# A decoder layer on one core: attention loads issued one per step, and late modulation computed by halves of 512 columns

## The chip, the cores and the metric

The kernel runs on one core of one Trainium2 chip. The metric is device time of one execution, in microseconds (us); smaller is better. The core has TensorE (PE, with its weight loads shown apart as PEld), VectorE (DVE), ScalarE (ACT), GpSimd (POOL) and SyncE (SP). SP issues nearly all the transfers between HBM and on-chip memory in this kernel; its queue is in order, so a row that waits holds every row behind it.

## The reference

The layer has 2048 tokens of width 1024, in float32, for a single sequence. Cut to what matters here:

```python
mod = silu(c) @ w_ada + b_ada          # w_ada is 1024 x 6144
shift_a, scale_a, gate_a, shift_m, scale_m, gate_m = split(mod, 6)
h = rms_norm(x, g_attn) * (1 + scale_a) + shift_a
q_f, k_f, v_f, q_s, k_s, v_s, f_logit = split(h @ w_in)
o_fox = forgetting_attention(q_f, k_f, v_f, log_sigmoid(f_logit + b_fgate))
o_sb = stick_breaking_attention(q_s, k_s, v_s)
mix = concat(head_rms_norm(o_fox), head_rms_norm(o_sb))
x = x + gate_a * (mix @ w_out)
h = rms_norm(x, g_mlp) * (1 + scale_m) + shift_m
x = x + gate_m * (conv_gated_mlp(h))
return rms_norm(x, g_final)
```

There are 8 forgetting ("fox") heads and 8 stick-breaking ("sb") heads of 64 columns, both causal. The six parts of `mod` are used at different times. The first two are needed before anything else. `gate_a` scales the output projection, so it can be multiplied into `w_out` beforehand. `scale_m`, `shift_m` and `gate_m` are wanted only after attention. The change touches how these last four are computed while attention runs.

## The kernel before, in words

Values that need full precision are split into a high and a low part, and a product is three matmuls (high by high, high by low, low by high).

**Units.** Attention is cut into 32 units, in this order: for sb and then for fox, four pairs of heads `p`, and for each pair four blocks `tb` of 512 tokens. A unit's attention (`attend`, L692) is the main stream. The projection of a later unit (`proj`, L455 on) runs as a filler between its steps: `follow` advances it as far as a table `pace` asks. The projection reads the normalised input in eight tiles of 512 KB for each block of tokens (the loads at L468, `hp<-hs`, matmuls at L342), multiplies them with the input weights and writes q, k and v back to HBM.

**Loads of a unit.** Once a unit's projection is done, `load_unit` (L351 to L365) issues the nine loads of its attention: four of Q (L362), four of K (L363) and one of V (L364). All nine come at one step.

**Late modulation.** From unit 12 on, `late_mod` (L757) is a second filler with 3 of its steps per unit. For each of four 1024-column parts of `w_ada` it takes a tile `wsum` and then, for each of the eight row blocks, a further tile `w`. It loads 512 KB (L776), and by halves of 512 columns scales them on ScalarE (L782) and adds them to `wsum` on GpSimd (L783); the first block is scaled on GpSimd straight into `wsum` (L780). A matmul with ones (L790) then sums over the partitions. For the two gates the bias row comes by a load of its own into a tile `gt` (L787), which VectorE adds (L791). For the first gate `fold_out` (L743) multiplies `w_out` by it, splits the product and writes it to HBM. The second gate is stored from `gt` by one transfer (L796, `gate_m`).

**The ring.** All these tiles, `wsum`, `w`, `gt`, the raw and split tiles of `fold_out`, and the eight `hs` tiles of a projection, come from one ring of ten buffers of 512 KB (`h_tile`, L156; `wide` is the same buffer seen as 1024 columns). A load into a buffer waits until all users of its previous content are done.

**Order.** The rows of each engine are put in order by a planner that simulates the program. What a row waits for on the chip is decided by semaphores, and the order of rows on an engine is fixed.

## Time and profile before

| | us |
|---|---|
| median of 3 runs (lowest, highest) | 2948.92 (2948.36, 2949.31) |
| profiled execution, span | 2941.4 |
| TensorE busy in it | 2867.8 (97%) |
| VectorE, ScalarE, GpSimd busy | 2179.5, 1686.0, 901.1 |

The profiled execution's own span is 2941.4 us; the device time of the runs, 2948.92 us, also holds what lies around the span, 7.5 us. A sum made in the profile is therefore carried over by adding 7.5 us.

Rows name the source line, the engine, the operation, the tile written and the tile read. "hp" is a tile of the ring, "hs" the normalised input in HBM. "SPq" rows are the issues of transfers by SP. A wait "A <- B" says that engine row A stood idle until B released it. The PEclk column is the TensorE clock that was granted, as a share of full speed.

### The profile page before, as it was taken

To read this page: it belongs to the slowest core of one execution; us is meant where nothing else is said; L and a number is where in the kernel's file an instruction comes from. 1 tells how busy PE (TensorE), PEld (TensorE's weight loads), DVE (VectorE), ACT (ScalarE), POOL (GpSimd) and SP (SyncE) were. 2 spreads that over 40 slices of the span, in tenths; PEclk is the share of its full clock that TensorE was granted. 3 is DMA by queue.
4 is the path that set the end of the run, shared out by engine and by line. 5 is a ranking of instruction groups with operands and counts; after the bars stand their busy time and mean duration, and the time that the engine had idled before them with its cause. 6 is when DMAs were issued, how large, how long until landed. Compare 5 with 4: busy or idle time off the path is not lost.

```text
span 2941.4 us, 45922 instructions
## 1 busy us (share of the span) xinstructions
PE 2867.8 (97%) x15772; PEld 2459.7 (84%) x15772; DVE 2179.5 (74%) x3464; ACT 1686.0 (57%) x3187; POOL 901.1 (31%) x967
## 2 busy tenths in 40 slices
PE   8999999999999999999999999999999999999998
PEld 7888888888988988888888788888788888888887
DVE  5787778877886656658843788888998888575476
ACT  5776767677776656658744554444444445433342
POOL 0431322243032423231213344444254543142200
PEclk8999999999999999999999999999999999999999
DMA  9749756867469794794537775554754444975644
GB/s 293 255 139 321 236 188 207 301 211 229 162 212 356 269 277 139 232 323 140 182 120 233 245 232 128 130 136 129 236 132 125 130 130 132 309 257 185 216 158 151
DMA packets 348346, 601.89 MB, mean 205 GB/s; under 512 B 34672, under 2 KB 178800, under 8 KB 348112
## 3 DMA queue, kind: packets, MB, share of 16 engines
q1 hardware_dynamic: 324208, 558.06, 57.7%
q0 software_dynamic: 10880, 20.97, 4.3%
q10 hardware_dynamic: 13024, 19.93, 1.9%
q8 instruction: 124, 2.03, 0.3%
q14 instruction: 110, 0.90, 0.1%
HBM read 420.77 MB, written 177.02 MB: 203 GB/s over the span
## 4 chain that ended last, share of the span: by engine, by line
PE 46%; DMA 3%; DVE 2%; SPq 1%; ACT 1%; issue 1%; POOL 0%; DVEq 0%; ACTq 0%; POOLq 0%
PE ps_o L1315 19%; PE ps_t L1315 7%; PE ps_o L1614 6%; PE ps_t L1614 3%; PE ps_bc L1614 3%; PE ps_o L912 1%; PE ps_pv L615 1%; DMA r<-rstd 1%; PE ps_bc L912 1%; PE ps_pt L606 1%; PE ps_o L1609 1%; DMA wo<-wos 1%; DMA hm<-hf_m 1%; SPq L895 1%; DVE op L46 1%
## 5 line engine op out<-in xcount | busy, mean ns | idle before, releaser
L1315 PE MATMUL ps_o<-op,wu 128*128 128x512 f32 x2592 | 608.0, 389 | 2.0 <-DVE snap L1366 1.5
L1315 PEld LDWEIGHTS ps_o<-op,wu 128*128 128x128 f32 x2592 | 486.2, 188 | 103.9 <-DVE snap L1366 1.9
L611 DVE TENSOR_TENSOR at<-ps_pt,at 128x512 fp32r<-128x512 f32 (+1 forms) x576 | 366.1, 652 | 100.2 <-ACT at L610 97.3
L636 DVE TENSOR_TENSOR_SCAN a<-r,a 128x512 f32<-128x512 f32 (+2 forms) x320 | 368.3, 1167 | 77.8 <-ACT a L631 39.9
L342 PE MATMUL ps_pj<-hp,w_qk 128*128 128x512 f32 x1512 | 411.2, 403 | 14.5 <-DMA hp<-hs 12.9
L610 ACT ACTIVATE at<-ps_pt 128x512 fp32r<-128x512 f32 (+1 forms) x576 | 318.5, 576 | 139.1 <-PE ps_pt L606 123.1
L615 PE MATMUL ps_pv<-at,V 128*128 128x256 f32 x2216 | 386.8, 292 | 9.3 <-DVE at L611 4.2
L615 PEld LDWEIGHTS ps_pv<-at,V 128*128 128x128 f32 x2216 | 320.9, 190 | 39.8 <-DVE at L611 11.4
L342 PEld LDWEIGHTS ps_pj<-hp,w_qk 128*128 128x128 f32 x1512 | 275.4, 190 | 71.0 <-DMA hp<-hs 16.2
L45 ACT ACTIVATE wu<-wuraw 128x512 fp32r<-128x512 f32 x204 | 128.9, 632 | 248.5 <-PE ps_o L1315 190.1
L596 PE MATMUL ps_qk<-K,Q 128*128 128x512 f32 (+2 forms) x640 | 265.7, 416 | 5.6 <-ACT a L631 3.3
L413 PE MATMUL ps_pj<-w_v,hp 128*128 128x256 f32 (+1 forms) x1536 | 236.6, 288 | 2.1 <-DVE hp L422 1.6
L597 PE MATMUL ps_qk<-K,Q 128*128 128x512 f32 (+2 forms) x640 | 235.7, 369 | 0.0
L1315 PE MATMUL ps_t<-op,wu 128*128 128x512 f32 x888 | 220.8, 390 | 1.0 <-DVE op L46 1.0
L413 PEld LDWEIGHTS ps_pj<-w_v,hp 128*128 128x128 f32 x1536 | 209.0, 189 | 10.9 <-DVE q L373 1.5
L630 ACT ACTIVATE r<-ps_qk 128x512 f32<-128x512 f32 (+2 forms) x320 | 173.1, 541 | 58.2 <-PE ps_qk L597 55.5
L46 DVE TENSOR_TENSOR wu<-wuraw,wu 128x512 fp32r<-128x512 f32 x204 | 189.6, 930 | 18.1 <-ACT wu L45 16.7
L1315 PEld LDWEIGHTS ps_t<-op,wu 128*128 128x128 f32 x888 | 166.4, 188 | 36.5 <-DVE op L46 1.8
L606 PE MATMUL ps_pt<-edge,a 128*128 128x128 f32 x1088 | 185.1, 274 | 8.4 <-DVE a L636 7.8
L1614 PE MATMUL ps_o<-op 128*128 128x512 f32 x840 | 191.5, 389 | 0.0
L1614 PEld LDWEIGHTS ps_o<-op 128*128 128x128 f32 x840 | 157.7, 188 | 32.7
L679 ACT ACTIVATE p<-p,mn 128x128 f32<-128x128 f32 (+15 forms) x128 | 153.9, 1203 | 53.3 <-DVE mn L675 52.2
(342 smaller groups left out, 5237.6 us busy)
## 6 DMA issues: line engine op xcount, KB each, us to landing
hp<-hs SPq DMA_DIRECT2D x224, 512.0 KB
wuraw<-in_w_up_dram SPq DMA_DIRECT2D x80, 512.0 KB
ra<-g SPq DMA_DIRECT2D x136, 256.0 KB
rb<-in_w_down_dram SPq DMA_DIRECT2D x108, 256.0 KB
g<-u SPq DMA_DIRECT2D x80, 256.0 KB
hs<-hp SPq DMA_DIRECT2D x32, 512.0 KB
hp<-in_w_ada_dram SPq DMA_DIRECT2D x32, 512.0 KB
qk_fox<-q SPq DMA_DIRECT2D x32, 512.0 KB
```

Source lines behind the costliest of these rows:

```text
L46: (lo_engine or nc.gpsimd).tensor_sub(lo, src, f(hi))
L342: nc.tensor.matmul(acc, w[kt][:, a, n], h[:, bb], start=kt == 0 and i == 0, stop=kt == KT - 1 and i == 2)
L413: nc.tensor.matmul(av[:, t * width:(t + 1) * width], hts[kt][:, a, tok], w[1][kt][:, bb, 0:width], start=kt == 0 and m == 0, stop=kt == KT ...
L596: nc.tensor.matmul(b[:, :cw], Q[:, hl, 0, qcols], K[:, hl, :cw], start=True, stop=False)
L597: marks.append(nc.tensor.matmul(b[:, :cw], Q[:, hl, 1, qcols], K[:, hl, :cw], start=False, stop=True).ins)
L606: nc.tensor.transpose(b[:, i * P:(i + 1) * P], blk(kts[kk], qi), ident)
L610: copies = [nc.scalar.activation(at[:, 0, lo:], b[:, lo:], AF.Copy).ins, nc.vector.tensor_sub(at[:, 1, lo:], b[:, lo:], f(at[:, 0, lo:])).ins]
L611: nc.vector.tensor_sub(at[:, 1, lo:], b[:, lo:], f(at[:, 0, lo:])).ins]
L615: m = nc.tensor.matmul(o[:, 0:2 * P], V[kt // 4][:, kt % 4, hl, :], rhs, start=first and kk == 0 and w == 0, stop=last and kk == 1 and w == 1)
L636: nc.vector.tensor_tensor_scan(rev, r[:, 0:need][:, ::-1], rev, 0.0 if right[qi] is None else right[qi][:, 0:1], ALU.mult, ALU.add)
L1315: nc.tensor.matmul(b, w[:, p, j], o[:, q], start=first and i == 0, stop=last and i == 2, skip_group_check=True)
L1614: nc.tensor.matmul(b, a[:, p, t * P:(t + 1) * P], w[:, q], start=first and i == 0, stop=last and i == 2, skip_group_check=True)
```

## The change

Two things change. `load_unit` no longer issues its nine transfers but puts them in a list; `arrive`, called at every attention step, issues one of them, or all that remain when few steps are left in the unit (`n - m` not above the list's length plus six). Late modulation works on 512 columns at a time: one ring tile (`two_`) holds `wsum` in its first half and `w` in its second, all eight loads (256 KB each) go into the same `w`, and the gate's bias and the gate itself take `w`'s place after them. `fold_out` is called once for each half, uses the `wsum` half for the raw `w_out` rows, and takes one further tile at a time for the split. The filler gets 5 steps per unit rather than 3, since it now has about 90 steps in place of 55.

```diff
--- before.py
+++ after.py
@@ -359,10 +359,16 @@
             rows = slice(h * HD, (h + 1) * HD)
             for r in range(2):
                 half = slice(r * HD, (r + 1) * HD)
-                nc.sync.dma_start(f(Q[half, h]), src[rows, 0])
-                nc.sync.dma_start(f(K[half, h]), src[rows, 1, r])
-        nc.sync.dma_start(f(V), vs[kind][p][tb])
+                arriving.append((f(Q[half, h]), src[rows, 0]))
+                arriving.append((f(K[half, h]), src[rows, 1, r]))
+        arriving.append((f(V), vs[kind][p][tb]))
         res.append((Q, K, V))
+
+    arriving = []
+
+    def arrive(n):
+        for _ in range(min(n, len(arriving))):
+            nc.sync.dma_start(*arriving.pop(0))
 
     def finish_proj(kind, p, tb, aq, w, hts, ak=None):
         direct = (kind, p) == ("sb", 0)
@@ -740,18 +746,15 @@
         nc.sync.dma_start(os_[mp][tb], oT)
         yield
 
-    def fold_out(gt):
+    def fold_out(n, gt, raw):
+        sl = slice(n * TB, (n + 1) * TB)
         for kt in range(KT):
-            raw = wide()
-            nc.sync.dma_start(raw, w_out[kt * P:(kt + 1) * P, :])
-            for n in range(2):
-                sl = slice(n * TB, (n + 1) * TB)
-                nc.vector.scalar_tensor_tensor(raw[:, sl], raw[:, sl], cols[:, R_GF + kt:R_GF + kt + 1], gt[:, sl],
-                                               ALU.mult, ALU.mult)
-                w = h_tile()
-                split(w[:, 0], w[:, 1], raw[:, n * TB:(n + 1) * TB])
-                nc.sync.dma_start(wos[kt][:, :, n * TB:(n + 1) * TB], f(w))
-                yield
+            nc.sync.dma_start(raw, w_out[kt * P:(kt + 1) * P, sl])
+            nc.vector.scalar_tensor_tensor(raw, raw, cols[:, R_GF + kt:R_GF + kt + 1], gt, ALU.mult, ALU.mult)
+            w = h_tile()
+            split(w[:, 0], w[:, 1], raw)
+            nc.sync.dma_start(wos[kt][:, :, sl], f(w))
+            yield
 
     def late_mod():
         cr = f(h_tile())[0:2 * NFULL + 1].rearrange("p a (b n) -> p (a b) n", b=4)[:, 0:4]
@@ -770,37 +773,37 @@
         yield
         late = ((2, 0), (5, 1), (3, None), (4, None))
         for part, gate in late:
-            wsum = wide()
-            for kt in range(KT):
-                w = wide()
-                nc.sync.dma_start(w, w_ada[kt * P:(kt + 1) * P, part * D:(part + 1) * D])
-                for n in range(0, D, 512):
-                    sl = slice(n, n + 512)
+            for n in range(2):
+                two_ = f(h_tile())
+                wsum, w = two_[:, 0], two_[:, 1]
+                sl = slice(part * D + n * TB, part * D + (n + 1) * TB)
+                for kt in range(KT):
+                    nc.sync.dma_start(w, w_ada[kt * P:(kt + 1) * P, sl])
                     if kt == 0:
-                        nc.gpsimd.tensor_scalar_mul(wsum[:, sl], w[:, sl], cs[:, 0:1])
+                        nc.gpsimd.tensor_scalar_mul(wsum, w, cs[:, 0:1])
                     else:
-                        nc.scalar.activation(w[:, sl], w[:, sl], AF.Copy, scale=cs[:, kt:kt + 1])
-                        nc.gpsimd.tensor_add(wsum[:, sl], wsum[:, sl], w[:, sl])
-                yield
-            if gate is not None:
-                gt = wide()
-                nc.sync.dma_start(gt, b_ada[0:1, part * D:(part + 1) * D].to_broadcast([P, D]))
-                for n in range(2):
+                        nc.scalar.activation(w, w, AF.Copy, scale=cs[:, kt:kt + 1])
+                        nc.gpsimd.tensor_add(wsum, wsum, w)
+                    yield
+                if gate is not None:
+                    nc.sync.dma_start(w, b_ada[0:1, sl].to_broadcast([P, TB]))
                     b = pt()
-                    nc.tensor.matmul(b, ones, wsum[:, n * 512:(n + 1) * 512], start=True, stop=True)
-                    nc.vector.tensor_add(gt[:, n * 512:(n + 1) * 512], b, gt[:, n * 512:(n + 1) * 512])
+                    nc.tensor.matmul(b, ones, wsum, start=True, stop=True)
+                    nc.vector.tensor_add(w, b, w)
                     yield
-                if gate == 0:
-                    yield from fold_out(gt)
+                    if gate == 0:
+                        yield from fold_out(n, w, wsum)
+                    else:
+                        nc.sync.dma_start(gate_m[:, n * TB:(n + 1) * TB], w)
                 else:
-                    nc.sync.dma_start(gate_m, gt)
-            else:
-                cb = pt()
-                for d in range(KT):
-                    nc.tensor.matmul(cb[:, d:d + 1], wsum[:, d * P:(d + 1) * P], ones[:, 0:1], start=True, stop=True)
-                i = 1 if part == 3 else 0
-                nc.vector.tensor_add(mod_m[:, i], cb[:, 0:KT], cols[:, R_BA + part * KT:R_BA + (part + 1) * KT])
-                yield
+                    cb = pt()
+                    for d in range(KT // 2):
+                        nc.tensor.matmul(cb[:, d:d + 1], wsum[:, d * P:(d + 1) * P], ones[:, 0:1], start=True, stop=True)
+                    i = 1 if part == 3 else 0
+                    d0 = n * KT // 2
+                    c0 = R_BA + part * KT + d0
+                    nc.vector.tensor_add(mod_m[:, i, d0:d0 + KT // 2], cb[:, 0:KT // 2], cols[:, c0:c0 + KT // 2])
+                    yield
         nc.vector.scalar_tensor_tensor(mod_m[:, 0], mod_m[:, 0], 1.0, cols[:, R_GM:R_GM + KT], ALU.add, ALU.mult)
         yield
 
@@ -859,7 +862,7 @@
                       base + (total - base) * (done + weight(units[i]) * m / n) / span if i >= START else 0)
 
     LAG, ENDQ = 12, 16
-    LATE, PER = 12, 3
+    LATE, PER = 12, 5
     START, STOP = 3, 30
 
     HT = 2 * P
@@ -1020,6 +1023,7 @@
     weights["sb", 0], results["sb", 0] = load_w("sb", 0), []
     first_block(weights["sb", 0])
     load_unit(*units[0], results["sb", 0])
+    assert not arriving
     loaded_units = [1]
     close_pool("mod")
     sx = open_pool("sx", side="right")
@@ -1063,6 +1067,7 @@
             if nxt and projected[1] > i + 1 and loaded_units[0] == i + 1:
                 loaded_units[0] += 1
                 load_unit(*nxt, results[nxt[:2]])
+            arrive(1 if n - m > len(arriving) + 6 else len(arriving))
 
         interleave(attend(kind, p, tb, results[kind, p], Fbs), n, [(lm if i >= LATE else None, PER, False), (tail, 17 + IDLE if nxt is None else 13, True)], follow)
         while nxt and loaded_units[0] == i + 1:
```

In the changed kernel the line numbers are higher: the loads of a unit are at L371, of `hs` at L474, of `w_ada` at L781, the bias at L789 and the store of `gate_m` at L797.

The following rows are from SP's order, in which "x4" stands for four transfers in a row and the number behind a name tells tiles apart. First the place where late modulation begins (sb units), before:

```order
L316 DMA raw_qk_8414<-in_w_in_dram 128x2x128
L776 DMA hp_8615<-in_w_ada_dram 128x1024
L394 DMA qk_sb3_3_8202<-q2_8319 128x1024
L316 DMA raw_v_8419<-in_w_in_dram 128x256
L316 DMA raw_v_8424<-in_w_in_dram 128x256
L776 DMA hp_8671<-in_w_ada_dram 128x1024
L316 DMA raw_v_8429<-in_w_in_dram 128x256
L316 DMA raw_v_8434<-in_w_in_dram 128x256
```

and with the change:

```order
L316 DMA raw_qk_8414<-in_w_in_dram 128x2x128
L781 DMA hp_8614<-in_w_ada_dram 128x512
L474 DMA hp_9201<-hs1_0_68 128x1024
L400 DMA qk_sb3_3_8202<-q2_8319 128x1024
L316 DMA raw_v_8419<-in_w_in_dram 128x256
L781 DMA hp_8614<-in_w_ada_dram 128x512
L316 DMA raw_v_8424<-in_w_in_dram 128x256
L316 DMA raw_v_8429<-in_w_in_dram 128x256
L316 DMA raw_v_8434<-in_w_in_dram 128x256
```

Before, each load of `w_ada` goes to a new ring buffer; now every load goes to `hp_8614`, and an `hs` load has come between.

Next the place where attention turns to fox pair 1 and the projection of fox pair 2, token block 1, begins (tiles `hs1`), before:

```order
L363 DMA K_13512<-qk_fox1_2_12345 64x512 x3
L653 DMA Fb_13244<-fs_243 128x1024
L362 DMA Q_13260<-qk_fox1_1_11941 64x1024 x4
L440 DMA vs_fox2_0_222<-q2_13722 128x1024
L440 DMA vs_fox3_0_226<-q2_13723 128x1024
L363 DMA K_13989<-qk_fox1_3_12746 64x512 x4
L468 DMA hp_14078<-hs1_5_73 128x1024
L468 DMA hp_14107<-hs1_6_74 128x1024
L468 DMA hp_14112<-hs1_7_75 128x1024
L776 DMA hp_14199<-in_w_ada_dram 128x1024
```

and with the change, where the first `hs1` load is the row of `hp_14006`:

```order
L781 DMA hp_13439<-in_w_ada_dram 128x512
L371 DMA K_14660<-qk_fox2_0_13236 64x512 x2
L316 DMA raw_qk_16521<-in_w_in_dram 128x2x128
L371 DMA V_14018<-vs_fox1_3_221 128x1024
L316 DMA raw_qk_16526<-in_w_in_dram 128x2x128
L316 DMA raw_qk_16531<-in_w_in_dram 128x2x128
L474 DMA hp_14006<-hs1_0_68 128x1024
L789 DMA hp_12309<-in_b_ada_dram 128x512
L474 DMA hp_14011<-hs1_1_69 128x1024
L474 DMA hp_14057<-hs1_2_70 128x1024
L474 DMA hp_14062<-hs1_3_71 128x1024
L474 DMA hp_14093<-hs1_4_72 128x1024
```

Before, the sixth to eighth `hs1` tiles stand behind Q, two stores of v and four K loads; now the K and V loads stand ahead of the whole block, mixed with loads of `w_ada`, and the bias row of the gate stands behind the first `hs1` load.

Last the end of the loads for the projection of fox pair 2, token block 3 (tiles `hs3`), before, where `gate_m` is the store of the second gate:

```order
L653 DMA Fb_15445<-fs_243 128x1024
L362 DMA Q_15461<-qk_fox2_1_14178 64x1024 x3
L363 DMA K_15722<-qk_fox2_2_14948 64x512
L796 DMA gate_m_248<-hp_14928 128x1024
L363 DMA K_15722<-qk_fox2_2_14948 64x512
L468 DMA hp_15772<-hs3_7_91 128x1024
L364 DMA V_15463<-vs_fox2_1_223 128x1024
L776 DMA hp_15866<-in_w_ada_dram 128x1024
```

and with the change:

```order
L781 DMA hp_15551<-in_w_ada_dram 128x512
L371 DMA Q_14659<-qk_fox2_0_13236 64x1024 x4
L446 DMA vs_fox2_2_224<-q2_15346 128x1024
L446 DMA vs_fox3_2_228<-q2_15347 128x1024
L474 DMA hp_15785<-hs3_6_90 128x1024
L474 DMA hp_15790<-hs3_7_91 128x1024
L781 DMA hp_15551<-in_w_ada_dram 128x512
```

Before, the eighth tile `hs3_7` follows the store of `gate_m`, whose tile is a ring buffer; now both halves of that store come earlier in the order, and the eighth `hs3` tile follows the seventh. Ahead of the block stand single-tile loads of `w_ada` (`hp_15551`), four of them in a row:

```order
L797 DMA gate_m_248<-hp_13439 128x512
L386 DMA qk_fox2_2_14970<-q2_14967 128x1024
L781 DMA hp_15551<-in_w_ada_dram 128x512
L400 DMA qk_fox2_2_14970<-q2_15130 128x1024
L781 DMA hp_15551<-in_w_ada_dram 128x512 x4
L474 DMA hp_15595<-hs3_0_84 128x1024
L474 DMA hp_15600<-hs3_1_85 128x1024
L474 DMA hp_15677<-hs3_2_86 128x1024
```

On SP there are 1824 issue rows in place of 1781: the loads of `w_ada` go from 32 to 64, of `w_out` from 8 to 16, of the bias from 2 to 4, and `gate_m` is stored in two pieces. The number of rows on TensorE, ScalarE and GpSimd is the same; VectorE has two more. The first row that differs is 3815 of 15555 on TensorE, 955 on ScalarE, 199 on GpSimd and 224 on SP.

## The prediction

> **What bounds the kernel now.** I read the page first, then what TensorE waits for in the whole span and in the stretch where late modulation runs beside fox attention, then the timeline at its longest gaps, the stage windows around them, and SP's queue, which feeds them.
>
> ```profile
> span 2941.4 us, 45922 instructions
> PE 2867.8 (97%) x15772; PEld 2459.7 (84%) x15772; DVE 2179.5 (74%) x3464; ACT 1686.0 (57%) x3187; POOL 901.1 (31%) x967
> ```
>
> TensorE is busy for 97% of the span. Of the other 73.6 us only what lies in this stage can be had, plus what lies hidden in busy time at a lower clock. The waits in the whole span, then those from 880 to 1500 us:
>
> ```profile
> PE ps_pj L342 <- DMA hp<-hs: 12.9, 8, 6.0
> PE ps_pt L606 <- DVE a L636: 7.8, 16, 1.5
> PE ps_pv L615 <- DVE at L611: 4.2, 9, 1.0
> ...
> PE ps_pj L342 <- DMA hp<-hs: 9.9, 3, 6.0
> PE ps_bc L615 <- ACT at L610: 1.4, 3, 0.6
> ```
>
> So three waits for `hs` tiles make 9.9 us, and two of them are nearly all of it. The timeline has them, with the idle time before each in brackets; the row between is the last projection ahead of the second:
>
> ```profile
> 1052.80 2.93 PE L342 MATMUL ps_pj<-hp,w_qk 128*128 128x512 f32 x6 [6.01 <-DMA hp<-hs]
> ...
> 1155.19 1.66 PE L342 MATMUL ps_pj<-hp,w_qk 128*128 128x512 f32 x6 [0.47 <-DMA hp<-hs]
> 1208.81 2.93 PE L342 MATMUL ps_pj<-hp,w_qk 128*128 128x512 f32 x6 [3.40 <-DMA hp<-hs]
> ```
>
> After each the clock is down. The windows give length, busy time with counts of PE, PEld, DVE, ACT and POOL, granted clock, DMA share and GB/s:
>
> ```profile
> 1052.80:1056.40 3.60, 3.60 (x11) 2.91 (x12) 0.00 (x0) 0.00 (x0) 0.00 (x0) 0.50 1.06 308
> 1208.80:1213.60 4.80, 4.79 (x16) 4.21 (x17) 1.55 (x3) 3.11 (x10) 0.74 (x1) 0.50 0.76 290
> 880.00:900.00 20.00, 19.99 (x123) 17.17 (x121) 14.43 (x38) 13.83 (x32) 6.72 (x10) 1.00 1.04 374
> 1020.00:1040.00 20.00, 20.00 (x136) 17.94 (x135) 13.53 (x34) 14.87 (x29) 8.33 (x10) 1.00 1.00 285
> 1160.00:1180.00 20.00, 19.80 (x142) 18.05 (x142) 18.64 (x51) 16.60 (x27) 3.39 (x6) 1.00 0.04 15
> ```
>
> Half clock for 3.60 and 4.80 us costs 1.8 and 2.4 us of work. The stalls are then worth 6.0 + 1.8 = 7.8 and 3.4 + 2.4 = 5.8, together 13.6 us, 0.46% of the span. This is the pool from which a gain can come.
>
> [...]
>
> Why were the tiles late? SP's issues around the stalls (start, time, line, transfer, count):
>
> ```profile
> 1041.12 4.49 SPq L363 DMA_DIRECT2D K<-qk_fox  x4
> 1045.92 2.54 SPq L468 DMA_DIRECT2D hp<-hs  x3
> ...
> 1087.76 0.73 SPq L787 DMA_DIRECT2D hp<-in_b_ada_dram  x1
> ...
> 1154.17 1.04 SPq L316 DMA_DIRECT2D raw_qk<-in_w_in_dram  x2
> 1167.74 0.34 SPq L740 DMA_DIRECT2D os<-oT  x1
> 1181.77 1.72 SPq L653 DMA_DIRECT2D Fb<-fs  x2
> 1189.81 3.01 SPq L363 DMA_DIRECT2D K<-qk_fox  x5
> ...
> 1198.70 0.33 SPq L796 DMA_DIRECT2D gate_m<-hp  x1
> 1199.07 0.44 SPq L363 DMA_DIRECT2D K<-qk_fox  x1
> 1200.74 0.33 SPq L468 DMA_DIRECT2D hp<-hs  x1
> ```
>
> The first stall is a load issued too late on full transfer engines (share 1.00 from 1020 on): the three `hs` tiles are issued behind four K loads and land only at 1052.80, 6.9 us after the first of them. The second is the ring: `gt` was taken with the bias load at 1087.76 and left with the `gate_m` store at 1198.70, 111 us later; the next issue but one is the eighth `hs` tile, on which TensorE waits. In between the transfer engines were all but idle (0.04 from 1160 to 1180), so nothing but a buffer and an in-order queue stood in the way.
>
> **The change part by part.**
>
> *The ring, second stall.* Before, late modulation holds `wsum`, `gt` and a `w` in flight, each a whole buffer; now one buffer at a time for half a part (two when two halves overlap), and no `gt`. In SP's order all eight `hs3` tiles stand together, and `gate_m`'s stores come before them. Both causes are gone: minus 3.4 + 2.4 = 5.8 us. If the tile is late anyway for the queue, 0 to 5.8 comes back; I take all of it as won.
>
> *The unit's loads, first stall.* Spreading holds only where the unit has more steps left than loads plus six. Before unit 12 it does next to nothing: up to there SP's order differs by one K load that moved behind a store of q. From the fox pairs on, the K, V and Q loads stand mixed with `w_ada` loads and ahead of the `hs1` block rather than inside it. Ahead of `hs1_0` there are still K, V and raw weights. TensorE waits on no K, Q or V load in the rows shown, so moving them earlier costs nothing by itself; what matters is whether the block of eight `hs` loads lands in time. Bounds: the stall is gone (minus 7.8) or it moves to the block's first tile at about its old size (0). The queue shows 4.49 us for four K loads; taking those out from between would leave 6.0 - 4.5 = 1.5 us of the 6.0, but the block's 4 MB at the 285 GB/s shown is 14.7 us, so its last tiles are less safe than its first. I keep about two thirds of the stall, 5.0 us, as the cost of a smaller stall here or at the next pair, and so win 2.8.
>
> *The stage in the sb units,* where late modulation starts:
>
> ```profile
> 560.00:640.00 80.00, 77.53 (x463) 66.68 (x462) 60.36 (x76) 56.72 (x123) 14.84 (x19) 1.00 0.74 255
> 640.00:720.00 80.00, 73.45 (x474) 63.42 (x473) 58.16 (x78) 59.02 (x134) 38.50 (x44) 1.00 0.79 232
> ...
> PE ps_pt L606 <- DVE a L636: 3.6, 7, 1.1
> PE ps_pv L615 <- DVE at L611: 2.9, 6, 1.0
> PE ps_pj L342 <- DMA hp<-hs: 2.4, 4, 1.0
> ```
>
> TensorE idles 9.0 us in these 160 us; the last three rows are its waits from 600 to 880. Only the third is about the ring; I take 2.0 of its 2.4 as won. Bounds: 4 lost, if moved rows meet the vector chain at a worse place (about what the first row cost already), to 7 won.
>
> *The chain of single loads.* Late modulation's rows:
>
> ```profile
> L776 SPq DMA_DIRECT2D hp<-in_w_ada_dram x32: 328/333/2012, 629.7 to 1308.4; - x32
> L782 ACT ACTIVATE hp<-hp,cs x56: 705/714/744, 643.8 to 1320.8; 128x512 f32<-128x512 f32 x56
>   DMA hp<-in_w_ada_dram: 23.5, 17
> L783 POOL TENSOR_TENSOR hp<-hp x56: 1267/1293/2204, 644.6 to 1322.3; 128x512 f32<-128x512 f32 x56
> L780 POOL TENSOR_SCALAR hp<-hp,cs x8: 1557/1567/1574, 637.1 to 1251.3; 128x512 f32<-128x512 f32 x8
>   DMA hp<-in_w_out_dram: 2.2, 3
> ```
>
> Scaling and adding are of the same shape and number, so their busy time does not change. What changes is the wait: `w` is one buffer, so a load is issued only after the add before it, and ScalarE meets each of 56 loads singly instead of every second instruction of a pair. It waited 23.5 us in 17 of them; queued behind such a wait are the exponentials and scalings of attention (L610) for TensorE. If exposures double, ScalarE waits another 23.5. What reaches TensorE is bounded by 0 and that 23.5. The nearest row is TensorE's own: 1.4 us for L610 from 880 to 1500. I take it once more, with the extra waits of VectorE's `w_out` loads (2.2 us before) for another 0.6: plus 2.0. For the range I use 0 and 8, a third of the upper end, since ScalarE is busy for 57%.
>
> *SP and the transfers.* 43 more issues at 333 ns are 14 us over the 690 us in which late modulation runs, in a queue that stood idle in the stretch above; hidden. Uncovered, four more issues ahead of an `hs` block are 1.3 us. Value 0, bounds 0 to 2.
>
> [...]
>
> *Sum:* -5.8 - 2.8 - 2.0 + 2.0 + 0 = -8.6 us. From 2941.4 that is 2932.8, and with the 7.5 us by which the runs' median stands above the span, 2940.3; I write 2940.5. All units after about 1320 us are untouched, and late modulation's last add at 1322.3 is not on TensorE's way, so what is won remains won.
>
> **The rivals.**
>
> *Exchange.* The two stalls go and others of their kind come: the order now puts the whole `hs1` block behind K, V and `w_ada` loads, and the same at the turn to fox pair 2. For it: full transfer engines at 1020 to 1060, which the change relieves of nothing (the same bytes). Against it: the second stall had idle transfer engines. Two stalls of 7.8 and 5.8 become two of 5 to 8 us: 2948.9 - 13.6 + 13 = 2948. The variant in which the change does not do what it says, the loads not being spread where it counts, ends at the same figure.
>
> *The single-buffered chain holds SP (slower).* Each load waits for GpSimd's add, and SP holds everything behind it. One link is the landing, the scaling and the add. The first load above was issued at 629.7 and used at 637.1, so a link is up to 7.4 + 0.7 + 1.3 = 9.4 us. 64 + 16 such links would take 752 us against the 693 from 629.7 to 1322.3. The place is SP's order before the `hs3` block: four loads into `hp_15551` in a row, 4 x 9.4 = 38 us in which no `hs` load can be issued. Attention alone covered 52 us between 1156 and 1208 before; that cover is now cut into shorter pieces. From a link of about 8 us on (4 x 8 = 32) it decides. Priced by the stall of the same kind, three places of this form (ahead of `hs1`, `hs2`, `hs3`) cost 3 x 7.8 = 23.4 where 13.6 was paid before: 2948.9 + 9.8, about 2959. Against it: links in an idle stretch should be shorter, and two chains overlap in parts of the order.
>
> **How the numbers follow.** I give the forecast 0.48, the exchange 0.27, the chain 0.25. The forecast's own range, from its bounds, is 2933 to 2946 (all of the first stall won and 7 in the sb stage gives 2930.6; 0 there and the chain's 8 gives 2949; neither end is likely whole). With the exchange and most of the chain's case the range is 2931 to 2958. A measurement of this kernel can tell about 0.2% from no change, 5.9 us: faster is below 2943.0, slower above 2954.8. Faster holds most of the forecast's case (0.41) and a little of the exchange (0.06): 0.47. Same: 0.07 + 0.18 + 0.04 = 0.29. Slower: 0.03 of the exchange and 0.21 of the chain: 0.24.
>
> **What would show it.** Right: no wait of L342 on `hp<-hs` above 2 us between 1150 and 1250 and a granted clock of 1.00 there; at most one such wait near 1040 to 1060, below 5 us; ScalarE's wait for `w_ada` grown without TensorE's wait on L610 growing by more than 2 us. Exchange: new waits of 3 us or more on `hp<-hs` at other times with windows at 0.50 behind them. The chain: SP's waits for the `w_ada` buffer on GpSimd's add far above what they were, and `hs` issues right behind them. The forecast is wrong altogether if the time is gained or lost outside 620 to 1330 us, or if TensorE waits on late modulation's own matmuls.

## The result: slower, 1.0042 of the time before

The changed kernel takes 2965.31 us in the median of 7 runs (2950.13 to 2968.64), the kernel before 2948.92 (2948.35 to 2956.09). The ratio is 1.0042, with a 95% interval of 1.0025 to 1.0060. So about 12 us were lost by the ratio, 16 by the medians, where 8 had been forecast as a gain.

The page of the changed kernel, its first lines:

```profile
span 2963.6 us, 45975 instructions
PE 2879.3 (97%) x15772; PEld 2466.2 (83%) x15772; DVE 2170.2 (73%) x3466; ACT 1685.6 (57%) x3187; POOL 906.6 (31%) x967
```

TensorE executes as many instructions as before, yet is busy 11.5 us longer (2879.3 against 2867.8) and idle 10.7 us longer (84.3 against 73.6). The mean granted clock over the span fell from 0.993 to 0.990, which makes some 8.6 of the 11.5 us. That part is chance: in a second pair of traces, shown further down, the clock is 0.988 before and 0.991 with the change, and TensorE is busy equally long (2877.6 and 2877.4 us). What both pairs share is more idle time, in the second pair 80.7 us against 75.7. The profiled execution of the changed kernel took 2965.31 us with a span of 2963.6, so only 1.7 us lie around a span. The 7.5 us that the prediction put there were for the most part chance: the profiled execution of before was a quick one.

TensorE's waits in the changed kernel (what waited, for what, total us, times, longest):

```profile
PE ps_pj L342 <- DMA hp<-hs: 9.4, 8, 2.4
PE ps_pt L612 <- DVE a L642: 7.5, 16, 1.5
PE ps_pj L419 <- ACT w_v L45: 5.3, 2, 2.8
PE ps_pv L621 <- DVE at L617: 5.2, 9, 1.8
```

No stall of 6 us is left, and the longest wait for an `hs` tile is 2.4 us. But their sum is still 9.4 us (12.9 before), and a wait for ScalarE's split weights is new. The timeline has these places, and one more, ahead of 922.27 us:

```profile
922.27 1.48 PE L621 MATMUL ps_pv<-at,V 128*128 128x256 f32 x9 [1.99 <-DVE oT L744]
...
1047.78 0.50 PE L419 MATMUL ps_pj<-w_v,hp 128*128 128x256 f32 x2 [2.80 <-ACT w_v L45]
1054.47 0.50 PE L419 MATMUL ps_pj<-w_v,hp 128*128 128x256 f32 x2 [2.54 <-ACT w_v L45]
...
1257.74 1.63 PE L342 MATMUL ps_pj<-hp,w_qk 128*128 128x512 f32 x3 [2.43 <-DMA hp<-hs]
```

The windows of the changed kernel (length, busy us with counts of PE, PEld, DVE, ACT and POOL, granted clock, DMA share, GB/s) from 890 to 1000, and around the two stalls of before:

```profile
890.00:1000.00 110.00, 104.71 (x640) 90.34 (x639) 80.81 (x211) 70.04 (x131) 27.72 (x38) 0.97 0.74 252
1040.00:1060.00 20.00, 14.19 (x99) 13.03 (x99) 6.94 (x14) 9.55 (x23) 6.05 (x9) 0.91 0.92 231
1150.00:1250.00 100.00, 99.06 (x645) 88.36 (x644) 54.53 (x137) 54.82 (x97) 25.54 (x33) 1.00 0.70 236
1250.00:1265.00 15.00, 12.57 (x84) 11.53 (x84) 7.64 (x17) 7.42 (x16) 1.47 (x2) 0.89 1.05 246
```

and of before, for the first:

```profile
890.00:1000.00 110.00, 109.92 (x670) 96.80 (x669) 74.53 (x178) 66.76 (x128) 33.60 (x44) 1.00 0.91 329
```

From 890 to 1000 us, where TensorE had been busy without a gap, it now idles 5.3 us and runs at a mean clock of 0.97 (110 x 0.03 = 3.3 us more). These are the first units of fox attention, whose rows are short. What fills TensorE there is shown by the same windows for the projection's bank `ps_pj` alone (PE, PEld, DVE, ACT), before:

```profile
890.00:1000.00 110.00, 56.73 (x224) 39.50 (x223) 6.88 (x10) 5.96 (x10) 1.00 0.91 329
```

and after:

```profile
890.00:1000.00 110.00, 29.38 (x114) 20.73 (x115) 3.95 (x6) 3.24 (x6) 0.97 0.74 252
```

224 projection matmuls stood between the attention's steps, now 114. The longest gap there, the 1.99 us for `oT`, has a second side, in VectorE's timeline:

```profile
921.13 0.75 DVE L753 SCALAR_TENSOR_TENSOR hp<-hp,cols 128x512 f32<-128x512 f32 x1 [1.69 <-DMA hp<-in_w_out_dram]
921.80 0.41 DVE L744 TENSOR_TENSOR oT<-ps_pv,o 64x256 f32<-64x256 f32 x1
```

L753 is a row of `fold_out`, a part of late modulation. VectorE waited 1.69 us in it for a load of `w_out`, and the row that TensorE needed stands right behind it in VectorE's order. In the kernel before, ten such rows run in this stretch and none of them waits.

Two explanations went to the experiments. **Theory A**: the single `w` buffer; its loads hold ScalarE's and SP's in-order queues (VectorE's, shown above, was not in it). **Theory D**: the order that the planner makes of the changed program uses the projection up too early, and where it is missing the chain of attention (scores, maximum, exponential, sum) lies open. Beside them stands **theory B**, that the spread loads cost, and **theory C**, chance in the landing of transfers.

### The profile page after: what moved, and what is told of

The parts are those of the page before. It is cut to its first block, busy times and chain, and to the rows that moved or that the text cites. A ratio compares the mean times of both kernels' runs of the same rounds, so it can differ in the third digit from the quotient of the medians.

```text
span 2963.6 us, 45975 instructions
## 1 busy us (share of the span) xinstructions
PE 2879.3 (97%) x15772; PEld 2466.2 (83%) x15772; DVE 2170.2 (73%) x3466; ACT 1685.6 (57%) x3187; POOL 906.6 (31%) x967
## 5 line engine op out<-in xcount | busy, mean ns | idle before, releaser
L342 PE MATMUL ps_pj<-hp,w_qk 128*128 128x512 f32 x1512 | 414.8, 403 | 13.6 <-DMA hp<-hs 9.4
L642 DVE TENSOR_TENSOR_SCAN a<-r,a 128x512 f32<-128x512 f32 (+2 forms) x320 | 366.1, 1161 | 80.7 <-ACT a L637 39.8
L342 PEld LDWEIGHTS ps_pj<-hp,w_qk 128*128 128x128 f32 x1512 | 274.1, 190 | 69.7 <-DMA hp<-hs 13.0
L602 PE MATMUL ps_qk<-K,Q 128*128 128x512 f32 (+2 forms) x640 | 267.3, 419 | 10.7 <-ACT a L637 4.5
L46 DVE TENSOR_TENSOR op<-ra,op 128x512 fp32r<-128x512 f32 x144 | 108.5, 759 | 95.9 <-ACT op L45 93.3
```

The source lines that it names most:

```text
L46: (lo_engine or nc.gpsimd).tensor_sub(lo, src, f(hi))
L342: nc.tensor.matmul(acc, w[kt][:, a, n], h[:, bb], start=kt == 0 and i == 0, stop=kt == KT - 1 and i == 2)
L602: nc.tensor.matmul(b[:, :cw], Q[:, hl, 0, qcols], K[:, hl, :cw], start=True, stop=False)
L642: nc.vector.tensor_tensor_scan(rev, r[:, 0:need][:, ::-1], rev, 0.0 if right[qi] is None else right[qi][:, 0:1], ALU.mult, ALU.add)
```

## The experiments

All ratios are against runs of the kernel before on the same chip, with 95% intervals.

**How far chance goes.** The changed kernel and the kernel before were run once more, unchanged.

> The changed kernel once more, for a second trace. It lost about 5.5 us against before ahead of late modulation's start, where the order of rows is the same on every engine but for one K load, about 13 us in the stage of late modulation and about 4 us in the MLP. If chance in the landing of transfers makes the parts ahead and behind (theory C), they are at other places or gone in this trace, and the losses in the stage of late modulation stay: ScalarE waits for w_ada around 50 us in all, and the two TensorE stalls on ScalarE's w_v of 2.5 to 2.8 us come again. If all is set by the order, the same gaps stand at the same places and the time is 2965 within 2 us.

> The kernel before once more, for a second trace. The stalls at 1052 (about 6 us) and 1208 (about 3.4 us) should stand again if they are set by the order; idle time from 890 to 1000 us should be below 1 us again. Parts outside late modulation (300 to 600 us, and the MLP after 1720) show how far chance alone moves them, 2 to 4 us each.

Measured: the change again 2962.60 us, 1.0050 (1.0032 to 1.0068). The copy of before 2953.88 us, 1.0012 (0.9999 to 1.0025), with a span of 2953.3 in its profiled execution against 2941.4 in the first. So differences of 0.1% are nothing here, and one trace of this kernel can differ from another by 12 us. In the second trace of the change the losses that count stand again: 6.6 us idle from 890 to 1000 at a clock of 0.97, the two waits on `w_v` (shorter, 1.9 and 1.7 us), 50.8 us of ScalarE's waits for `w_ada`. In the second trace of before the two stalls stand again (4.53 us at 1063, 3.33 us at 1219), and 890 to 1000 us is again without a gap (109.92 busy). Theory C is out as a cause, though it blurs every small difference.

**The spread loads alone.** The edit on the kernel before is the list and `arrive` only:

```diff
-                nc.sync.dma_start(f(Q[half, h]), src[rows, 0])
-                nc.sync.dma_start(f(K[half, h]), src[rows, 1, r])
+                arriving.append((f(Q[half, h]), src[rows, 0]))
+                arriving.append((f(K[half, h]), src[rows, 1, r]))
...
+            arrive(1 if n - m > len(arriving) + 6 else len(arriving))
```

> The kernel before with only the spreading of a unit's nine loads. Theory A (late modulation's single buffer holds ScalarE's and SP's queues): the time of before within 0.2%, 2943 to 2955, and ScalarE's wait for w_ada stays at 20 to 30 us. Theory B (the spread loads fall into bursts at the turns between fox pairs and make the weights and hs tiles late): slower by 8 us or more, with stalls near the turns. The second stall of before (ring held by the gate tile) should stay under both.

Measured: 2962.21 us, 1.0036 (1.0022 to 1.0051). So the half of the change that the prediction costed at nothing is slower by itself, as theory B expected and theory A did not. From 1150 to 1250 us TensorE is busy 89.8 of 100 us, where the two traces of before have 95.6 and 95.8. TensorE's timeline has this wait:

```profile
1159.53 1.65 PE L342 MATMUL ps_pj<-hp,w_qk 128*128 128x512 f32 x6 [2.49 <-DMA hp<-hs]
```

and SP's, ahead of it:

```profile
1150.24 2.37 SPq L371 DMA_DIRECT2D Q<-qk_fox  x4
1152.71 0.53 SPq L474 DMA_DIRECT2D hp<-hs  x1
```

Before, the same place read:

```profile
1151.16 0.34 SPq L468 DMA_DIRECT2D hp<-hs  x1
1151.70 1.73 SPq L362 DMA_DIRECT2D Q<-qk_fox  x3
```

The `hs` load now comes behind the four Q loads, and the wait grows from the 0.47 us that the prediction quotes to 2.49. The second stall of before stands again, as expected, with 4.51 us at 1210, and one more follows (2.99 us at 1244).

**The halves alone.** The change with `arrive(len(arriving))`, which issues all nine loads at once again:

> The change with a unit's nine loads issued all at once again, as before; late modulation by halves. Theory A: as slow as the whole change, 2955 to 2968, with ScalarE's wait for w_ada at 45 us or more. Theory B: back to 2943 to 2955. If both parts are needed for the loss, it lies between.

Measured: 2967.95 us, 1.0054 (1.0034 to 1.0073). Theory A's and D's part is there without the spread loads: 7.3 us idle from 890 to 1000, with 147 projection matmuls. The two parts do not add up (0.36% and 0.54% alone, 0.42 to 0.50% together), and each has an order of its own.

**Against the single buffer: three `w` tiles.**

```diff
-                wsum, w = two_[:, 0], two_[:, 1]
+                wsum, w0 = two_[:, 0], two_[:, 1]
+                ex = f(h_tile())
...
                 for kt in range(KT):
+                    w = (w0, ex[:, 0], ex[:, 1])[kt % 3]
...
+                    w = w0
```

> The whole change, but w goes round three half tiles (one more buffer of the ring), so that a load need not wait for the add before it. Theory A: ScalarE's wait for w_ada falls to 25 us or less, SP's wait for the w_ada buffer on the add from 71 to 20 us or less, and the time falls by 6 us or more against the change in the same call. Against theory A: the waits fall but the time stays within 3 us of the change.

Measured: 2962.40 us, 1.0031 (1.0015 to 1.0046). ScalarE's wait for `w_ada` went from 54.0 to 21.9 us and SP's wait for the add from 71.4 to 36.2, half of it rather than the 20 expected. By the ratios the time is lower than the change's by 0.1 to 0.2%, inside the intervals; by the medians taken beside each other (2962.40 and 2962.60) it is the same. The 6 us that theory A expected are not there. From 890 to 1000 it still idles 4.4 us, with 140 projection matmuls.

**ScalarE freed: the scaling on GpSimd.**

```diff
-                        nc.scalar.activation(w, w, AF.Copy, scale=cs[:, kt:kt + 1])
+                        nc.gpsimd.tensor_scalar_mul(w, w, cs[:, kt:kt + 1])
```

> The whole change, with the scaling of w_ada moved from ScalarE to GpSimd (56 more rows of about 1.57 us there), so that ScalarE never waits for a load of w_ada. Theory A (ScalarE's in-order queue held by single loads is what costs): ScalarE's wait for w_ada goes from 51 to 54 us to 0, the stalls on w_v near 1040 shrink, and the time falls by 6 us or more against the change (2962 to 2965). Theory D (with the ring free, the projection keeps up with its pace and is used up, so that TensorE has attention alone from about 890 to 975 us, where each wait of the attention chain shows): the time stays within 4 us of the change and the idle time of that stretch stays.

Measured: 2961.24 us, 1.0032 (1.0017 to 1.0046). ScalarE waits for `w_ada` no more (GpSimd now waits 88.6 us for it). From 1040 to 1060 us TensorE is busy 16.9 of 20 us at full clock, against 14.2 at 0.91 in the first trace of the change, or 16.1 at full clock in the second (there from 1030 to 1050). So theory A is right about the two waits on `w_v`, worth between 1 and 4.5 us there, but not about the 6 us. From 890 to 1000 the idle time stays: 4.6 us, 130 matmuls.

**Most of the loads left out.** In this kernel 56 of the 64 loads of `w_ada`, and all 56 scalings and adds, are left out; the sums are of the first row block alone. The loads of `w_out` stay.

> The whole change without seven of the eight loads, scalings and adds of each half part of late modulation: 56 of 64 loads of w_ada and all 56 scalings and adds are left out, and the sums are of the first row block alone. Theory A: 2930 to 2945, the stalls on w_v and the losses of 890 to 1000 us gone with ScalarE's waits. Theory D: the dry stretch stands in the order as in the change, TensorE still loses 8 us or more from 890 to 1000 us, and the time is 2950 to 2962.

Measured: 2952.93 us, 1.0006 (0.9989 to 1.0022). So these loads, scalings and adds cost some 10 us of the changed kernel's time (what they cost the kernel before was not measured). The time lies inside what theory D expected, near its lower end, and not in theory A's 2930 to 2945; the 8 us or more that theory D expected from 890 to 1000 us were 5.8 us of idle time at full clock, with 143 projection matmuls. The stall behind the turn to fox pair 2 is longer than in the change:

```profile
1241.45 2.07 PE L342 MATMUL ps_pj<-hp,w_qk 128*128 128x512 f32 x4 [5.70 <-DMA hp<-hs]
```

So the stall at the turn is not made by the work on `w_ada`. For the dry stretch the run says less, because `fold_out` still runs there. Its longest wait, 2.73 us for `oT` ahead of 909.73, again stands right behind VectorE's row

```profile
908.59 0.75 DVE L753 SCALAR_TENSOR_TENSOR hp<-hp,cols 128x512 f32<-128x512 f32 x1 [2.43 <-DMA hp<-in_w_out_dram]
```

**The second stall by itself.** In the kernel before, the tile of the second gate alone is taken from another pool. This touches what the prediction named as the cause of the stall at 1208 us, and nothing earlier:

```diff
-                gt = wide()
+                gt = wide() if gate == 0 else px.tile([P, D], F32, name="xt", tag="xt", bufs=4)
```

> The kernel before with one thing changed: the tile of the second gate (bias and sum, stored as gate_m) comes from the pool of the x tiles and not from the ring. The order of TensorE's rows is the same up to the turn to fox pair 1's last block; there the dry stretch (6, 0, 0, 0 projection matmuls in four groups of 8 x QK) is filled (39, 51, 51, 36). If the second stall of before (3.4 us and half clock behind it, near 1208) comes from the ring held by that tile, it is gone: 3 to 6 us faster than before in the same call, and the stretch 890 to 1000 stays without idle time. Against that: the stall moves to the next hs block, time within 2 us of before.

Measured: 2955.29 us, 1.0016 (1.0005 to 1.0028), the same as the copy of before beside it (1.0012), and not the 3 to 6 us faster that were expected of the ring as the cause. The stall at 1208 is gone, and this is what came instead, in TensorE's timeline:

```profile
1241.82 2.63 PE L342 MATMUL ps_pj<-hp,w_qk 128*128 128x512 f32 x6 [3.75 <-DMA hp<-hs]
```

and in SP's:

```profile
1222.39 2.37 SPq L363 DMA_DIRECT2D K<-qk_fox  x4
...
1228.98 3.00 SPq L363 DMA_DIRECT2D K<-qk_fox  x5
1232.65 0.33 SPq L380 DMA_DIRECT2D qk_fox<-q  x1
1233.86 0.33 SPq L468 DMA_DIRECT2D hp<-hs  x1
1236.28 2.37 SPq L362 DMA_DIRECT2D Q<-qk_fox  x4
```

With the ring free, the projection is further on when attention turns to fox pair 2 (at 1233 us here, 1195 in the first trace of before), and there K, Fb and Q loads stand around the next `hs` load. The stall of before was 3.4 us at 1208, just behind its turn; this is 3.75 us at 1242, just behind the turn; the changed kernel's is 2.43 us at 1257, with its turn at 1244. It goes with the turn, and each time the transfer engines are full. These are the windows (length, busy us, granted clock, DMA share, GB/s as above) of before, of this kernel and of the change:

```profile
1200.00:1208.00 8.00, 5.41 (x46) 4.94 (x44) 5.73 (x13) 4.39 (x9) 1.07 (x2) 1.00 1.03 295
1234.00:1242.00 8.00, 4.25 (x34) 3.90 (x33) 4.80 (x14) 5.41 (x11) 1.10 (x3) 1.00 0.99 278
1244.00:1258.00 14.00, 11.57 (x76) 10.23 (x75) 6.49 (x16) 7.10 (x15) 2.18 (x4) 0.99 1.05 269
```

In the kernel before the awaited `hs` load was issued at 1200.74, and TensorE could use it at 1208.81, 8 us later. The ring's tile explained when the stall came, not whether.

**The ring at nine buffers.**

> The whole change with nine buffers in the ring rather than ten. If the ring's freedom is what lets the projection run ahead and dry up (theory D), a smaller ring moves the dry stretch but does not remove it: by the order of rows it still has one where the change has it (8 x QK groups 41 to 43 with 30, 0, 0 projection matmuls) and another later (57 to 59, as before the change), so 2960 to 2975. If instead late modulation's chain holds the queues (theory A), one buffer less adds waits for hs tiles on top: slower than the change by 5 us or more, in L342.

Measured: 2987.48 us, 1.0128 (1.0102 to 1.0154). One buffer less costs some 24 us against the change. That is outside theory D's 2960 to 2975 and agrees with theory A's 5 us or more, though its sign, waits for `hs` in L342, grew by only 3.8 us (13.2 against 9.4). 890 to 1000 stays dry (124 matmuls, 7.6 us idle), and from 760 to 890 us it idles 11.9 us where the change idles 3.5.

**Three orders meant to bring the projection back.** The pace table's weight of the sb units at 1.2 instead of 1.4; the planner's hold on the projection extended to unit 20 with a lag of 2; a ring buffer of its own for each tile of late modulation.

> The whole change with the weight of the sb units in the pace table at 1.2 rather than 1.4, so that more of the projection is left for the fox units; by the order of rows the groups 41 to 45 now have 55, 13, 0, 18, 30 projection matmuls, where the change has 6, 0, 0, 18, 30. Theory D: the idle time from 890 to 1000 us falls from 13 to 7 us or less, and the time by 5 to 10 us against the change, if nothing new opens at the start of late modulation. Theory A: no change within 4 us, since the loads of late modulation are the same.

> The whole change with the planner's rule that ties a projection step to a past attention matmul extended from unit 16 to unit 20 and its lag cut from 12 to 2 matmuls: the projection may not run ahead. By the order the groups 40 to 45 have 45, 24, 12, 0, 24, 24 projection matmuls. Theory D: idle time from 890 to 1000 us down to 9 or less; the whole time is less sure, since the rule also acts on the sb units. Theory A: idle time there unchanged.

> The whole change, but wsum, each w, the gate and each raw row block of w_out take a ring buffer of their own, as in the kernel before, of which only half is used; loads by halves, 5 steps per unit and the spread loads stay. Theory D: with the ring as scarce as before, the projection is held back; by the order the groups 41 to 46 have 24, 0, 24, 24, 33, 50 matmuls rather than 6, 0, 0, 18, 30, 0. Idle time from 890 to 1000 us falls from 12 to 14 us to 7 or less, and the time by 3 us or more against the change unless the scarce ring brings stalls on hs back elsewhere. If the halves themselves (twice as many loads, 256 KB each) cost the time, it stays at 12.

Measured: 2978.71 us, 1.0095 (1.0071 to 1.0118); 2976.13 us, 1.0098 (1.0078 to 1.0117); 2971.66 us, 1.0081 (1.0063 to 1.0099). All three are slower than the change, where theory D had expected the first to be faster, and the third too unless waits for `hs` came back (they are 12.3 us there against 9.4). In the first the stretch stayed dry on the chip (157 matmuls, 6.5 us idle). The other two lowered the idle time a little, to 4.2 and 3.4 us, with 150 and 175 matmuls, and idled more elsewhere: the one with the hold 10.8 us from 1300 to 1500 against 6.7 in the change, the one with its own tiles 9.2 us from 760 to 890 against 3.5.

**The sharing without the halves.** The kernel before with one `w` for a part's eight loads, the gate in `w`, the raw rows in `wsum`, all 1024 columns wide, 3 steps per unit:

```diff
             wsum = wide()
+            w = wide()
             for kt in range(KT):
-                w = wide()
...
-                gt = wide()
+                gt = w
```

> The kernel before with the sharing alone: late modulation takes one w tile for all eight loads of a part, the gate goes into w and the raw w_out rows into wsum, all at the full 1024 columns; no halves, 3 steps per unit, a unit's loads at once. It holds two ring buffers instead of up to five, and each load waits for the add before it. Theory A (the single-buffered chain costs): slower than before by 8 us or more. Theory D (only a dry stretch at the short fox units costs): by the order the groups 41 to 45 have 6, 36, 24, 24, 42 projection matmuls, so the idle time from 890 to 1000 us is below 3 us; the time is within 5 us of before (2945 to 2958), and the stalls at the turns of the fox pairs remain.

Measured: 2956.42 us, 1.0034 (1.0018 to 1.0050), about 0.2% above the copy of before. Against the kernel before itself that is 8 us by the medians and 10 by the ratio, so theory A's forecast of 8 us or more holds as well as theory D's range of times. A single buffer can thus be half of the loss or more; this run does not exclude it. 890 to 1000 us has 214 matmuls and 1.9 us of idle time, so a freed ring by itself does not dry the projection up. VectorE waits for `w_out` there too, once for 3.06 us:

```profile
956.06 1.42 DVE L749 SCALAR_TENSOR_TENSOR hp<-hp,cols 128x512 f32<-128x512 f32 x2 [3.06 <-DMA hp<-in_w_out_dram]
```

TensorE has projection at that time and waits for nothing from 950 to 960 us.

**Halves, with projection in that stretch.** Two runs keep the halves and the shared tile and change only the steps of late modulation: begun at unit 10, or 3 steps per unit.

> The whole change with late modulation started at unit 10 instead of 12. By the order of rows the groups 40 to 46 now have 43, 32, 34, 48, 44, 107, 42 projection matmuls (the change: 63, 6, 0, 0, 18, 30, 0), while groups 28 and 32 to 33, in the sb units, are dry instead. Theory D: idle time in the short fox units (890 to 1000 us) falls from 13 to 14 us to 3 or less, and idle time from 600 to 760 us, in the sb units, grows from 16 to 22 by 5 or more; the whole is near the change (2955 to 2970). If the halves themselves cost in the fox units (A, or the transfers), the idle time from 890 to 1000 us stays above 9.

> The whole change with 3 steps of late modulation per unit instead of 5 (what is left of it is done in one go before the last two units). By the order the groups 40 to 47 have 30, 12, 36, 47, 44, 44, 68, 37 projection matmuls (the change: 63, 6, 0, 0, 18, 30, 0, 36), and then groups 48 to 52, at the turn to fox pair 1, have none. Theory D: TensorE's waits on the attention chain (VectorE's maxima and sums) from 890 to 1000 us fall from 4.5 us to 1.5 or less, as they do not depend on the halves, and idle time of 5 us or more appears at the turn, between 1000 and 1100 us, beyond the 6 to 9 us of the other kernels. The whole is slower than the change (2970 or more). If the halves cost by themselves, the waits from 890 to 1000 us stay at 4 us or more.

Measured: 2984.46 us, 1.0129 (1.0111 to 1.0146), and 2966.26 us, 1.0061 (1.0040 to 1.0082). From unit 10, TensorE's waits from 890 to 1000 are

```profile
PE ps_pj L342 <- DMA hp<-hs: 2.9, 1, 2.9
PE ps_pj L419 <- DVE q L379: 1.2, 1, 1.2
```

and two of 0.3 us and less. Those on the attention chain, which the change had there (2.0 us for `oT`, 1.8 for `mn`, 1.2 for `at`), are gone, but an `hs` stall stands in their place, so the idle time of 4.7 us misses both forecasts. The idle time from 600 to 760 us grew as forecast, to 16.4 us from 10.2; the whole, at 2984.46 us, is far above the 2955 to 2970 forecast. With 3 steps the windows of the whole kernel are these:

```profile
890.00:1000.00 110.00, 109.83 (x696) 98.36 (x695) 62.70 (x162) 63.22 (x123) 30.86 (x45) 1.00 0.80 261
1000.00:1100.00 100.00, 86.53 (x558) 74.80 (x557) 73.94 (x198) 67.34 (x132) 21.70 (x37) 0.93 0.64 198
```

those of `ps_pj` alone:

```profile
890.00:1000.00 110.00, 62.10 (x280) 46.04 (x278) 6.15 (x10) 5.76 (x11) 1.00 0.80 261
1010.00:1080.00 70.00, 0.00 (x0) 0.00 (x0) 0.00 (x0) 0.00 (x0) 0.93 0.62 178
```

and TensorE's waits from 1000 to 1100 us:

```profile
PE ps_qk L602 <- DVE mn L681: 7.4, 2, 7.3
PE ps_pj L342 <- DMA hp<-hs: 2.4, 1, 2.4
PE ps_pv L621 <- DVE at L617: 1.9, 2, 1.7
```

With the same halves and the same single buffer, 280 projection matmuls stand in the stretch and the idle time is 0.2 us at full clock. From 1010 to 1080, around the turn to fox pair 1 and its short units, there are now none at all, and there TensorE waits 7.3 us at once for VectorE's maximum. But the maximum was late because VectorE waited for `w_out`:

```profile
1051.44 0.75 DVE L753 SCALAR_TENSOR_TENSOR hp<-hp,cols 128x512 f32<-128x512 f32 x1 [7.56 <-DMA hp<-in_w_out_dram]
```

In this kernel `fold_out` has moved too: none of its rows runs from 890 to 1000 us, and the last runs at 1119.5. From unit 10 it ends ahead of 890 us as well. So the gap moved together with the missing projection and with `fold_out`, and these two runs cannot part them. The whole is 2966 us where 2970 or more was forecast.

All kernels together, for 890 to 1000 us: projection matmuls (the count of `ps_pj`), idle time (110 minus TensorE's busy time), granted clock, and VectorE's wait for `w_out` ("none run" where no row of `fold_out` stands there).

| kernel | matmuls | idle us | clock | VectorE on `w_out`, us |
|---|---|---|---|---|
| before; again | 224; 216 | 0.1; 0.1 | 1.00; 1.00 | 0; 0 |
| spread alone; gate tile off the ring | 217; 216 | 0.1; 0.1 | 1.00; 1.00 | 0; 0 |
| shared at full width | 214 | 1.9 | 0.98 | 4.0 |
| halves, 3 steps | 280 | 0.2 | 1.00 | none run |
| halves from unit 10 | 259 | 4.7 (2.9 for `hs`) | 0.98 | none run |
| own tiles; slower pace; projection held | 175; 157; 150 | 3.4; 6.5; 4.2 | 0.99; 0.95; 0.98 | 5.3; 4.4; 4.0 |
| halves alone; without late loads; three w | 147; 143; 140 | 7.3; 5.8; 4.4 | 0.98; 1.00; 1.00 | 5.4; 5.5; 4.2 |
| scaling on GpSimd; the change again | 130; 126 | 4.6; 6.6 | 1.00; 0.97 | 3.8; 4.1 |
| ring of nine; the change | 124; 114 | 7.6; 5.3 | 0.97; 0.97 | 4.4; 3.1 |

Seven traces have more than 200 matmuls there, and but for the one with an `hs` stall they idle below 2 us; the ten with fewer idle 3.4 us and more.

The last column parts the kernels almost in the same way: the ten dry kernels all have VectorE waiting 3.1 to 5.5 us for `w_out` in the stretch, and of the others only the one at full width has. So two things meet in the dry stretch: VectorE is held by late modulation's loads, and there is little projection to run meanwhile. The 3.06 us at full width, hidden by projection, show that the first alone need not cost. That the second alone would, as theory D has it, no run shows, since no kernel without projection there is free of the waits. In the changed kernel 2.9 of the 5.0 us that TensorE's waits add up to in the stretch come right behind VectorE's waits for `w_out` (1.99 and 0.87 us), in its second trace 3.9 of 6.3 (2.78 and 1.10 us). What is left, 2.1 and 2.4 us in waits of less than 0.8 us, may be the open chain's own.

By time the theories stay open too: the kernels with halves lie at 1.0031 to 1.0129 as long as they keep their `w_ada` loads, those without halves at 1.0012 to 1.0036, and none with the halves that fills the stretch is faster than the change. That the halving itself costs is not excluded.

## Why the prediction was wrong

**The second stall was read in part only, and its removal was wrong.** The step that failed first is "Both causes are gone: minus 3.4 + 2.4 = 5.8 us ... I take all of it as won". The stall at 1208 did go with the tile, in the change and in the kernel with the gate tile off the ring. But the tile was one of two things that made the `hs` tile late; the other is the burst of K, Q and Fb loads at the turn to the pair, and the stall came back behind that turn (2.43 us and a clock of 0.89 over 15 us in the change, so 2.4 + 1.7 us). The prediction had ruled out the transfer engines by the window from 1160 to 1180 us, at a share of 0.04. From the issue of the `hs` load to its use, 1200 to 1208 us, the share was 1.03. Of the 5.8 us about 1.7 were won in the profile, and in the kernel that makes this step alone, none in time. The rival "exchange" had this mechanism, with the second stall named as the evidence against it.

**The first stall** was to be left at 5.0 us "here or at the next pair". What stands there is of another kind and somewhat larger: the two waits on `w_v` of 2.80 and 2.54 us, and a clock of 0.91 over 20 us (1.8 us). ScalarE's queue was held by two loads, one after the other, the first of the weights themselves and the second of `w_ada`, as its timeline in the changed kernel shows:

```profile
1047.31 0.42 ACT L45 ACTIVATE w_v<-raw_v 128x256 fp32r<-128x256 f32 x1 [3.56 <-DMA raw_v<-in_w_in_dram]
...
1053.14 0.72 ACT L785 ACTIVATE hp<-hp,cs 128x512 f32<-128x512 f32 x1 [3.78 <-DMA hp<-in_w_ada_dram]
```

**ScalarE's waits** were expected to double from 23.5 us; they were 54.0 in the changed kernel and 50.8 in its second trace. Where TensorE felt them, at the waits on `w_v`, the scaling on GpSimd puts their price between 1 and 4.5 us, within the bounds given (0 to 8).

**The spread loads** were costed at nothing, since "TensorE waits on no K, Q or V load ... so moving them earlier costs nothing by itself". That step looked at who waits for the moved loads and not at who stands behind them. Alone, they put an `hs` load behind four Q loads and made the kernel slower by 0.36%, of which the copy of before shows 0.12% to be nothing.

**The sb units** were to win 2.0 us. From 600 to 760 us TensorE idles 10.2 us in the change and 9.1 in its second trace; before it was 9.3 and 9.4. Nothing was won there.

**The term that was far too small** is "the extra waits of VectorE's `w_out` loads (2.2 us before) for another 0.6". It belongs to the largest loss, from 890 to 1000 us: 5.3 us idle and two stretches of 3.4 us at half clock (3.4 us of work lost), 6.6 and 3.4 in the second trace. VectorE's waits for `w_out` grew from 2.2 to 5.8 us in all (7.9 in the second trace). Right behind the two in this stretch TensorE waited 2.9 us (3.9), and each of the two half-clock stretches follows one of them. That is 6.3 us (7.3) where 0.6 stood. The price was taken from rows of before, where projection stood between the attention's steps. The sum had no term for that changing, because it took the rows of TensorE as unmoved when their number was the same; where the projection's matmuls stand among the attention's could have been counted in the order of rows beforehand. Which of the two, the later loads or the missing projection, would have cost how much alone stays open.

**The rival of the chain** had the sign, and with 2959 the nearest price, but not the place: SP did wait longer for the add (71.4 us against 23.2), and three tiles in place of one, which halved that, left the time within its interval. The four loads of one tile in a row, ahead of the `hs3` block, caused no stall in the first trace, where 1150 to 1250 us is 99.1 of 100 busy; in the second it is 94.9, with waits for `hs` of 1.74 us at 1210 and 3.36 at 1250. That a single buffer costs time all the same is what the sharing at full width suggests, and what VectorE's waits show by another queue than SP's.

**The sum, put right:** about 9 us lost from 890 to 1000. The two stalls of before were worth 14.9 rather than 13.6 us, since the granted clock stayed at 0.50 until 1057.8 and 1214.8, beyond the windows that the prediction read; 7.1 and 4.1 us are back in other form, so 3.7 won. Nothing was won in the sb units. That is about 5 of the 12 us; in the second pair of traces the same places give some 10 us lost and 2 won. What remains is of the size of chance between executions and is not settled. Why the planner's order for 5 steps dries the projection up where that for 3 does so one pair later was not found out either; no version that beats both kernels came out of these runs.

## What to carry to other kernels

Where a filler hides the latency of a chain, count where the filler's work will stand after a change, by place, and not only how much of it there is. Here 224 projection matmuls from 890 to 1000 us became 114; with 3 steps per unit in place of 5 the same halves had 280 there and none from 1010 to 1080. Look also for rows of other work in the queues of the engines that the chain runs on: in the changed kernel a row of `fold_out` on VectorE waited 1.69 us for its load, and TensorE waited 1.99 us for the row right behind it. A price taken beside a filler says little of a place where the filler is gone: at full width, with 214 projection matmuls in the stretch, VectorE waited 3.06 us in such a row while TensorE waited for nothing from 950 to 960 us. When a load was late for two reasons, ask what is left when one of them goes: of the 5.8 us taken for the stall at 1208, about 1.7 were won in the profile. A transfer that nobody waits for can still have its price in what stands behind it in the queue: with the loads spread alone, the `hs` load that came behind four Q loads was waited for 2.49 us rather than 0.47.

## What the hardware showed that was not expected

Half clock stood behind shorter waits than the stalls of 6.0 and 3.4 us that the prediction read. In the changed kernel TensorE waits 1.99 us for `oT` ahead of 922.27 us, in a stretch in which it is busy otherwise, and 0.87 and 0.40 us ahead of 965.21 and 966.12. Behind each place stands a stretch at half clock, though TensorE is busy throughout:

```profile
920.00:922.20 2.20, 0.28 (x2) 0.08 (x1) 1.06 (x3) 0.91 (x3) 0.00 (x0) 1.00 0.14 40
923.30:926.70 3.40, 3.40 (x15) 3.00 (x14) 1.89 (x6) 2.05 (x4) 1.03 (x2) 0.50 0.47 154
967.70:971.10 3.40, 3.40 (x17) 3.15 (x16) 2.67 (x8) 1.76 (x3) 0.00 (x0) 0.50 0.84 235
```

Each costs 3.40 x 0.50 = 1.7 us of work, against 2.5 us behind the 6 us stall of before (0.50 from 1052.8 to 1057.8, 5.0 us and not the 3.60 that the prediction read). But the length of a wait alone does not decide it: in the kernel without most of the late loads TensorE waits 2.73 us for the same tile, ahead of 909.73, and the granted clock from 890 to 1000 us is 1.00. What does decide it, these runs do not show.
